# Feed-forward products by Strassen's seven products in a kernel of two transformer blocks

## The chip, the cores and the metric

The kernel runs on one core of a Trainium2 chip as one program. The metric is the device time of one execution in microseconds (us), as a median of several runs; lower is better. PE is the matrix engine (TensorE), DVE the vector engine, ACT the scalar engine, POOL the GpSimd engine; SP issues the loads.

## What is computed

Two blocks follow each other on 512 tokens of 1024 features, in float32. Each has two gated feed-forwards around a token mixer (the mixers are left out here), and a small product follows at the end. A feed-forward normalises its input, takes 5632 columns of products from it (2816 "gate" and 2816 "up"), gates them and takes 1024 columns from those:

```python
def rms_norm(x, g):
    xf = x.astype(jnp.float32)
    y = xf * lax.rsqrt(jnp.mean(xf * xf, axis=-1, keepdims=True) + EPS)
    return (y * g.astype(jnp.float32)).astype(x.dtype)

def swiglu_ffn(x, w_in, w_out):
    gate, up = jnp.split(x @ w_in, 2, axis=-1)
    return (jax.nn.silu(gate) * up) @ w_out
```

The first block adds half of the normed result to x; the second adds half of the result. The four feed-forwards are called f1, f2 (block 1) and f3, f4 (block 2). Their order is f1, mixer, f2, f3, mixer, f4, and then the last product.

## The kernel before

Features lie on the 128 partitions, and the 512 tokens along the row. The input of a feed-forward is eight tiles of 128 features by 512 tokens, so a chunk of 128 columns of `w_in` takes eight steps k. A float32 product is made from parts: `split` (L306) and `wpiece` (L242) write a high part of an operand (a copy on ACT, L247 for weights, L310 and L313 for activations) and the rest, low, on DVE (L248 for weights, L311 and L314 for activations). `mm3` (L258) then issues three matmuls: high by high (L259), high weight by low input (L260), low weight by high input (L261).

`ffn` (L450) goes through 22 pairs m of a gate chunk and an up chunk. `lin` (L284) loads 512 KB of weights for a chunk on SP, makes the parts, and issues 24 matmuls of 512 columns into a PSUM bank, so a pair is 48 matmuls. The input parts are those of gain times x, without the per-token factor R, which arrives later (L393); R is multiplied in when DVE reads the bank (L463 and L464). ACT takes the Silu in place (L94), DVE multiplies gate and up (L466) and the product is split at once (L310, L311). Then the output products follow: `out_post` (L397) in f1 and f2, a loop at L472 in f3 and f4, eight chunks with 66 matmuls each (`f2o` for those of f2). The last chunk in f1 and f2 is done in two halves of 256 tokens.

The first two pairs of f1, f2 and f3 are issued ahead by `lin_ahead` (L295), also in halves of 256 columns, while the input still arrives; in f4 none is.

A tile scheduler orders the instructions of each engine by the data they need and the order in which they are written; the engines then run their lists strictly in order and wait on semaphores. Weights go through a pool of three raw buffers, four high and four low ones; other tiles of 128 by 512 come from a pool of 72. `Squares.add` (L367) sums squares on POOL (L376), which has no other large work. `late_constants` (L177) loads vectors of later stages on POOL's queue, transposes them into `pcolb`, and computes tables; in f1 it is written ahead of pair 2.

Tile names in the profile drop numbers: f_6g is the gate chunk of pair 6 in any of the feed-forwards (here the time tells which), `_r`, `_h`, `_l` are raw, high and low.

## Time and profile before

| | us |
|---|---|
| median of 3 runs (2273.32 to 2273.71) | 2273.33 |
| profiled execution, first to last instruction | 2267.5 |
| PE busy in it | 2247.1 (99%) |
| DVE busy | 1151.6 (51%) |
| ACT busy | 881.5 (39%) |
| POOL busy | 119.6 (5%) |

The span of the profiled execution is 5.8 us under the median of the times; a run's time takes in what lies before the first and behind the last instruction. The two are not told apart by the profile: differences of the span are set against the median as they are. The feed-forwards' pairs lie at 43 to 263 us (f1), 715 to 934 (f2), 1083 to 1302 (f3) and 1840 to 2082 (f4). Times of a matmul overlap: rows give a length of 0.39 us where one starts every 0.23 us, so what a matmul costs is read from start to start.

### The profile page before, as it was taken

To read this page: it belongs to the slowest core of one execution; us is meant where nothing else is said; L and a number is where in the kernel's file an instruction comes from. 1 tells how busy PE (TensorE), PEld (TensorE's weight loads), DVE (VectorE), ACT (ScalarE), POOL (GpSimd) and SP (SyncE) were. 2 spreads that over 40 slices of the span, in tenths; PEclk is the share of its full clock that TensorE was granted. 3 is DMA by queue.
4 is the path that set the end of the run, shared out by engine and by line. 5 is a ranking of instruction groups with operands and counts; after the bars stand their busy time and mean duration, and the time that the engine had idled before them with its cause. 6 is when DMAs were issued, how large, how long until landed. Compare 5 with 4: busy or idle time off the path is not lost.

```text
span 2267.5 us, 27653 instructions
## 1 busy us (share of the span) xinstructions
PE 2247.1 (99%) x11074; PEld 1870.9 (83%) x11074; DVE 1151.6 (51%) x1938; ACT 881.5 (39%) x1344; POOL 119.6 (5%) x156
## 2 busy tenths in 40 slices
PE   8999999999999999999999999999999999999999
PEld 7888888888788888889888888877778888888887
DVE  5644323778648444325644433476674654444334
ACT  4323223556635333223432322566654442233222
POOL 3000001000112000001000001000000010000000
PEclk9999999999889999999999999999999999999999
DMA  5333333322112333332333333321131233333331
GB/s 151 93 96 100 95 94 91 88 62 75 38 47 85 102 93 102 93 96 73 112 93 101 89 96 104 85 66 48 46 89 34 79 112 94 102 93 96 96 107 65
DMA packets 364836, 197.22 MB, mean 87 GB/s; under 512 B 10007, under 2 KB 356516, under 8 KB 364708
## 3 DMA queue, kind: packets, MB, share of 16 engines
q1 hardware_dynamic: 364100, 195.37, 30.0%
q8 instruction: 87, 1.43, 0.3%
q0 software_dynamic: 608, 0.09, 0.0%
q14 instruction: 41, 0.34, 0.0%
HBM read 193.33 MB, written 2.10 MB: 86 GB/s over the span
## 4 chain that ended last, share of the span: by engine, by line
PE 98%; DVE 1%; ACT 0%; DMA 0%; issue 0%; SPq 0%; DVEq 0%
PE f1o_p L260 2%; PE f2o_p L259 2%; PE f2o_p L260 2%; PE f1o_p L259 2%; PE f2o_p L261 2%; PE f1o_p L261 2%; PE f4o_p L259 2%; PE f3o_p L261 2%; PE f4o_p L261 2%; PE f3o_p L259 2%; PE f3o_p L260 2%; PE f4o_p L260 2%; PE gt_p L260 1%; PE gt_p L259 1%; PE gt_p L261 1%; PE f_p L260 1%
## 5 line engine op out<-in xcount | busy, mean ns | idle before, releaser
L248 DVE TENSOR_TENSOR f1o_l<-f1o_r,f1o_h 128x1024 fp32r<-128x1024 f32 (+1 forms) x24 | 27.3, 1136 | 76.6 <-ACT f1o_h L247 76.6
L248 DVE TENSOR_TENSOR f2o_l<-f2o_r,f2o_h 128x1024 fp32r<-128x1024 f32 (+1 forms) x24 | 27.3, 1136 | 76.6 <-ACT f2o_h L247 76.6
L247 ACT ACTIVATE f2o_h<-f2o_r 128x1024 fp32r<-128x1024 f32 (+1 forms) x24 | 23.8, 990 | 85.7 <-PE f2o_p L260 73.0
L247 ACT ACTIVATE f1o_h<-f1o_r 128x1024 fp32r<-128x1024 f32 (+1 forms) x24 | 23.8, 990 | 85.7 <-PE f1o_p L260 68.4
L247 ACT ACTIVATE f3o_h<-f3o_r 128x1024 fp32r<-128x1024 f32 (+1 forms) x24 | 23.8, 990 | 85.3 <-PE f3o_p L260 53.2
L247 ACT ACTIVATE f4o_h<-f4o_r 128x1024 fp32r<-128x1024 f32 (+1 forms) x24 | 23.8, 990 | 85.0 <-PE f4o_p L260 52.8
L376 POOL TENSOR_TENSOR f_acc<-f_acc,f_sq 128x256 f32<-128x256 f32 (+1 forms) x42 | 38.9, 927 | 316.9 <-ACT f_sq L375 299.5
L248 DVE TENSOR_TENSOR f3o_l<-f3o_r,f3o_h 128x1024 fp32r<-128x1024 f32 (+1 forms) x24 | 27.3, 1136 | 54.0 <-ACT f3o_h L247 54.0
L248 DVE TENSOR_TENSOR f4o_l<-f4o_r,f4o_h 128x1024 fp32r<-128x1024 f32 (+1 forms) x24 | 27.3, 1135 | 52.5 <-ACT f4o_h L247 52.5
L84 ACT ACT_TABLE_LOAD x36 | 46.2, 1283 | 1.4 <-PEq L1341 0.8
L376 POOL TENSOR_TENSOR m_acc<-m_acc,m_sq 128x256 f32<-128x256 f32 (+1 forms) x18 | 20.1, 1115 | 348.8 <-ACT m_sq L375 348.8
L260 PE MATMUL m1o_p<-mix_l,m1o_h 128*128 128x256 f32 (+1 forms) x88 | 29.3, 334 | 0.0
L261 PE MATMUL m1o_p<-mix_h,m1o_l 128*128 128x256 f32 (+1 forms) x88 | 29.2, 334 | 0.0
L259 PE MATMUL m1o_p<-mix_h,m1o_h 128*128 128x256 f32 (+1 forms) x88 | 28.6, 336 | 0.0
L376 POOL TENSOR_TENSOR pl_acc<-pl_acc,pl_sq 128x512 f32<-128x512 f32 x6 | 10.3, 1710 | 341.6 <-ACT pl_sq L375 341.6
L248 DVE TENSOR_TENSOR gt_l<-gt_r,gt_h 128x1024 fp32r<-128x1024 f32 x16 | 19.6, 1224 | 12.9 <-ACT gt_h L247 12.6
L94 ACT ACTIVATE l<-l 128x384 f32<-128x384 f32 (+1 forms) x48 | 24.2, 554 | 3.1 <-DVE l L949 3.0
L247 ACT ACTIVATE pg_h<-pg_r 128x1024 fp32r<-128x1024 f32 x8 | 8.5, 1061 | 42.6 <-PE pp L496 19.4
L94 ACT ACTIVATE e<-ms,mx,sck 128x512 f32<-128x512 f32 (+3 forms) x32 | 19.5, 614 | 14.0 <-DVE mx L1135 13.8
L260 PE MATMUL wo_p<-mg_l,wo_h 128*128 128x512 f32 x64 | 24.8, 390 | 0.0
L259 PE MATMUL wo_p<-mg_h,wo_h 128*128 128x512 f32 x64 | 24.8, 389 | 0.0
L376 POOL TENSOR_TENSOR f2p_acc<-f2p_acc,f2p_sq 128x512 f32<-128x512 f32 x6 | 7.7, 1288 | 322.9 <-ACT f2p_sq L375 322.9
(4287 smaller groups left out, 7533.5 us busy)
## 6 DMA issues: line engine op xcount, KB each, us to landing
f1o_r<-in_ffn_w_out_dram SPq DMA_DIRECT2D x16, 512.0 KB, 3.8
f2o_r<-in_ffn_w_out_dram SPq DMA_DIRECT2D x16, 512.0 KB, 4.3
f3o_r<-in_ffn_w_out_dram SPq DMA_DIRECT2D x16, 512.0 KB, 4.3
gt_r<-in_w_in_dram SPq DMA_DIRECT2D x16, 512.0 KB, 4.0
f4o_r<-in_ffn_w_out_dram SPq DMA_DIRECT2D x16, 512.0 KB, 4.1
f_r<-in_ffn_w_in_dram SPq DMA_DIRECT2D x12, 512.0 KB, 5.0
mg_r<-in_w_mix_in_dram SPq DMA_DIRECT2D x8, 512.0 KB, 4.0
m1o_r<-in_w_mix_out_dram SPq DMA_DIRECT2D x8, 512.0 KB, 4.2
```

The costliest lines, as they stand in the source:

```text
L84: ld = S.preload_act_table_set(name).ins
L94: i = S.activation(out, in_, func, **kw).ins
L247: S.activation(hi, raw, AF.Copy)
L248: V.tensor_tensor(lo, raw, hi.bitcast(F32), ALU.subtract)
L259: M.matmul(o, w[0], u[0], start=first, stop=False)
L260: M.matmul(o, w[0], u[1], start=False, stop=False)
L261: issued["last"] = M.matmul(o, w[1], u[0], start=False, stop=last).ins.name
L376: G.tensor_tensor(acc[:, sl], acc[:, sl], q[:, sl], ALU.add)
```

## The change

Pairs 0 to 5 of each feed-forward stay as they are (called direct). Pairs 6 to 21 are made by the Winograd form of Strassen's method: the weights of a pair and the input are cut into 2 by 2 blocks (k halves by gate and up; k halves by token halves), and seven products of blocks take the place of eight. A product of blocks is four steps k of three matmuls with 256 columns; a pair is 84 of these instead of 48 of 512.

The seven products need seven forms of the normed input (`b11`, `b21`, `n1`, `t3`, `t2`, `b22`, `t4`), each in four tiles with high and low parts. `strassen_input` makes them among the direct pairs: eight products of x, gain and R on DVE (the forms hold R, so R is not multiplied into the results), 16 sums and differences of 256 columns on DVE, 28 high parts on ACT and 28 low parts on DVE.

`strassen_pair` loads the two chunks of a pair raw (r0, r1), and makes four weight forms from them: a = r0, b = s1 (the two halves of r1 added, 512 columns), c = r0's first half added into r1, and d (s1 added into r0's first half, and that into its second half). The four additions, 128 by 512 each, are on POOL; of each form ACT makes the high part and DVE the low part. The results come together in two banks, `ab` and `cd`: ACT copies two halves (`s`), and DVE makes five sums of 256 columns (`o1`, `o2`). Silu and product of gate and up follow as before.

All 22 products are split behind the last pair and no longer pair by pair. `late_constants` is written behind the pairs of f1, `norm_post` is loaded at the very start on SP and taken out of it. There is one raw weight buffer more, and two tiles fewer in the pool.

```diff
+NDIRECT = 6
+HT = T // 2
+HK = KD // 2
...
-    act = ctx.enter_context(tc.tile_pool(name="act", bufs=72))
-    wraw = ctx.enter_context(tc.tile_pool(name="wraw", bufs=3))
+    act = ctx.enter_context(tc.tile_pool(name="act", bufs=70))
+    wraw = ctx.enter_context(tc.tile_pool(name="wraw", bufs=4))
...
     def late_constants():
-        load_rows(["norm_post", "ffn1_norm_2", "mix_norm_2", "ffn2_norm_2", "ple_norm_2", "hgrn_norm", "mlstm_norm",
+        load_rows(["ffn1_norm_2", "mix_norm_2", "ffn2_norm_2", "ple_norm_2", "hgrn_norm", "mlstm_norm",
                    "conv_w", "conv_b", "hgrn_lb_logits", "q_latent_norm_2", "kv_latent_norm_2"], "b", nc.gpsimd)
-        for i, j in ((0, 0), (1, 2)):
-            V.tensor_scalar(gph[:, i * KD:(i + 1) * KD], cols("norm_post", j * KD, KD), 0.5, None, ALU.mult)
         V.tensor_copy(identb, ident)
         ii, jj, xx, gt_ = (A(f"ix{i}", I32, (P, P)) for i in range(4))
...
+    def mm3(o, w, u, first, last, more=False):
...
+    def strassen_input(x, nx, R, between):
+        un, forms = [None] * KD, [{} for _ in range(HK)]
+        def normed(k):
+            un[k] = A(f"{nx.name}_n{k}")
+            V.scalar_tensor_tensor(un[k], x[k], nx.g(k), R, ALU.mult, ALU.mult)
+        def form(k, name, src, sign=1.0):
+            t = A(f"{nx.name}_{name}{k}", F32R)
+            hi, lo = t[:, 0:HT], t[:, HT:]
+            S.activation(hi, src, AF.Copy, scale=sign)
+            if sign > 0:
+                V.tensor_tensor(lo, src, hi.bitcast(F32), ALU.subtract)
+            else:
+                V.scalar_tensor_tensor(lo, src, sign, hi.bitcast(F32), ALU.mult, ALU.subtract)
+            forms[k][name] = hi, lo
+        between(0)
+        for k in range(KD):
+            normed(k)
+            form(k % HK, "b21" if k >= HK else "b11", un[k][:, 0:HT])
+        between(1)
+        d1, d2 = [], []
+        for k in range(HK):
+            b11, b12, b22 = un[k][:, 0:HT], un[k][:, HT:], un[HK + k][:, HT:]
+            d1.append(A(f"{nx.name}_d1{k}"))
+            V.tensor_tensor(d1[k][:, 0:HT], b12, b11, ALU.subtract)
+            V.tensor_tensor(d1[k][:, HT:], b22, b12, ALU.subtract)
+            form(k, "n1", d1[k][:, 0:HT], -1.0)
+            form(k, "t3", d1[k][:, HT:])
+        between(2)
+        for k in range(HK):
+            b21, b22 = un[HK + k][:, 0:HT], un[HK + k][:, HT:]
+            d2.append(A(f"{nx.name}_d2{k}"))
+            V.tensor_tensor(d2[k][:, 0:HT], b22, d1[k][:, 0:HT], ALU.subtract)
+            V.tensor_tensor(d2[k][:, HT:], d2[k][:, 0:HT], b21, ALU.subtract)
+            form(k, "t2", d2[k][:, 0:HT], -1.0)
+        between(3)
+        for k in range(HK):
+            form(k, "b22", un[HK + k][:, HT:])
+            form(k, "t4", d2[k][:, HT:])
+        return forms
 
+    def strassen_pair(w, c0, c1, forms, name, done):
+        r0, r1 = (wraw.tile([P, KD, P], F32, tag="raw", name=f"{name}_r{i}") for i in range(2))
+        for r, c in ((r0, c0), (r1, c1)):
+            nc.sync.dma_start(out=r, in_=w[:, c:c + P].rearrange("(k p) c -> p k c", p=P))
+        def parts(r, nm, n=KD):
+            if n == KD:
+                hi, lo = whi.tile([P, n, P], F32R, tag="hi", name=nm + "_h"), wlo.tile([P, n, P], F32R, tag="lo",
+                                                                                     name=nm + "_l")
+            else:
+                hi, lo = (act.tile([P, n, P], F32R, tag="a", name=f"{nm}_{j}") for j in "hl")
+            S.activation(hi, r, AF.Copy)
+            V.tensor_tensor(lo, r, hi.bitcast(F32), ALU.subtract)
+            return [(hi[:, k, :], lo[:, k, :]) for k in range(n)]
+        first, last = slice(0, HK), slice(HK, KD)
+        g1 = parts(r0, name + "a")
+        s1 = act.tile([P, HK, P], F32, tag="a", name=name + "_s1")
+        G.tensor_tensor(s1, r1[:, first], r1[:, last], ALU.add)
+        g2 = parts(s1, name + "b", HK)
+        G.tensor_tensor(r1[:, first], r0[:, first], r1[:, first], ALU.add)
+        g3 = parts(r1, name + "c")
+        G.tensor_tensor(r0[:, first], r0[:, first], s1, ALU.add)
+        G.tensor_tensor(r0[:, last], r0[:, last], r0[:, first], ALU.add)
+        g4 = parts(r0, name + "d")
+        def product(o, ws, form, start, stop, more=False):
+            for k in range(HK):
+                mm3(o, ws[k], forms[k][form], start and k == 0, stop and k == HK - 1, more)
+        ab, cd = ps(name + "_ab"), ps(name + "_cd")
+        (a, b), (c, d) = ((t[:, 0:HT], t[:, HT:]) for t in (ab, cd))
+        sab, o1, o2 = A(name + "_s"), A(name + "_o1"), A(name + "_o2")
+        product(a, g1[:HK], "b11", True, False)
+        product(b, g1[HK:], "b21", False, True)
+        yield
+        S.activation(sab[:, HT:], b, AF.Copy)
+        V.tensor_tensor(o1[:, 0:HT], a, sab[:, HT:], ALU.add)
+        product(c, g2, "n1", True, False)
+        product(d, g3[:HK], "t3", False, True)
+        product(a, g4[:HK], "t2", False, True, True)
+        S.activation(sab[:, 0:HT], a, AF.Copy)
+        V.tensor_tensor(o2[:, HT:], c, sab[:, 0:HT], ALU.add)
+        V.scalar_tensor_tensor(o2[:, HT:], o2[:, HT:], -1.0, d, ALU.mult, ALU.subtract)
+        yield
+        product(c, g4[HK:], "b22", False, False, True)
+        product(d, g3[HK:], "t4", False, True, True)
+        V.tensor_tensor(o1[:, HT:], c, sab[:, 0:HT], ALU.add)
+        V.scalar_tensor_tensor(o2[:, 0:HT], d, -1.0, sab[:, 0:HT], ALU.mult, ALU.subtract)
+        done(o1, o2)
+        yield
...
         us, R, _ = nx.factor()
         table("silu_and_others")
-        hs = []
-        for m in range(KF):
-            if m == 2 and name == "f1":
-                late_constants()
+        hs = [None] * KF
+        def direct(m):
             n = f"{name}_{m}"
-            pg = lin(w_in, m * P, us, n + "g")
-            pu = lin(w_in, DFF + m * P, us, n + "u")
-            gr, ur = A(n + "gr"), A(n + "ur")
+            return lin(w_in, m * P, us, n + "g"), lin(w_in, DFF + m * P, us, n + "u")
+        def gated(m, gr, ur):
+            lut(gr, gr, AF.Silu)
+            V.tensor_tensor(ur, gr, ur, ALU.mult)
+            hs[m] = ur
+        def evict(m, pg, pu):
+            gr, ur = A(f"{name}_{m}gr"), A(f"{name}_{m}ur")
             V.tensor_tensor(gr, pg, R, ALU.mult)
             V.tensor_tensor(ur, pu, R, ALU.mult)
-            lut(gr, gr, AF.Silu)
-            V.tensor_tensor(ur, gr, ur, ALU.mult)
-            hs.append(split(ur, n + "h"))
+            gated(m, gr, ur)
+        ready = {m: direct(m) for m in range(3)}
+        def between(i):
+            for m in ((0, 1), (2,), (3,), ())[i]:
+                evict(m, *ready.pop(m))
+            if i < 3:
+                ready[3 + i] = direct(3 + i)
+        forms = strassen_input(x, nx, R, between)
+        for m in range(4, NDIRECT):
+            evict(m, *(ready.pop(m) if m in ready else direct(m)))
+        pairs = {m: strassen_pair(w_in, m * P, DFF + m * P, forms, f"{name}_{m}",
+                                  lambda gr, ur, m=m: gated(m, gr, ur)) for m in range(NDIRECT, KF)}
+        run(pairs[NDIRECT], 1)
+        for m in range(NDIRECT, KF):
+            run(pairs[m], 1)
+            if m + 1 < KF:
+                run(pairs[m + 1], 1)
+            run(pairs[m])
+        hs = [split(hs[m], f"{name}_{m}h") for m in range(KF)]
+        if name == "f1":
+            late_constants()
...
-    load_rows(["norm_pre"], "a", nc.sync)
+    load_rows(["norm_pre", "norm_post"], "a", nc.sync)
+    for i, j in ((0, 0), (1, 2)):
+        V.tensor_scalar(gph[:, i * KD:(i + 1) * KD], cols("norm_post", j * KD, KD), 0.5, None, ALU.mult)
```

DVE's list in pairs 6 and 7 of f2 before: `gr` and `ur` are the products with R and then the gated product, `_l` the low parts of weights (8u, 9g, 9u, 10g) or of the gated product (6h, 7h).

```order
L248 TENSOR_TENSOR f2_8u_0_l_6525<-f2_8u_0_r_6522,f2_8u_0_h_6524 128x1024
L311 TENSOR_TENSOR f2_6h_l_6416<-f2_6ur_6410,f2_6h_h_6415 128x512
L463 TENSOR_TENSOR f2_7gr_6481<-f2_7g_p_6425,f2_R_6031 128x512
L248 TENSOR_TENSOR f2_9g_0_l_6566<-f2_9g_0_r_6563,f2_9g_0_h_6565 128x1024
L464 TENSOR_TENSOR f2_7ur_6482<-f2_7u_p_6456,f2_R_6031 128x512
L466 TENSOR_TENSOR f2_7ur_6482<-f2_7gr_6481,f2_7ur_6482 128x512
L248 TENSOR_TENSOR f2_9u_0_l_6597<-f2_9u_0_r_6594,f2_9u_0_h_6596 128x1024
L311 TENSOR_TENSOR f2_7h_l_6488<-f2_7ur_6482,f2_7h_h_6487 128x512
```

DVE's list now for one pair, from the low part of form d of pair 8 to that of pair 9 (`a_l` to `d_l` are low parts of weight forms, L569 is the product of gate and up):

```order
L515 TENSOR_TENSOR f2_8d_l_7691<-f2_8_r0_7669,f2_8d_h_7690 128x1024
L515 TENSOR_TENSOR f2_9a_l_7797<-f2_9_r0_7792,f2_9a_h_7796 128x1024
L569 TENSOR_TENSOR f2_7_o2_7575<-f2_7_o1_7574,f2_7_o2_7575 128x512
L545 TENSOR_TENSOR f2_8_o2_7698<-f2_8_cd_7695,f2_8_s_7696 128x256
L546 SCALAR_TENSOR_TENSOR f2_8_o2_7698<-f2_8_o2_7698,f2_8_cd_7695 128x256
L515 TENSOR_TENSOR f2_9b_l_7803<-f2_9_s1_7800,f2_9b_h_7802 128x512
L540 TENSOR_TENSOR f2_9_o1_7820<-f2_9_ab_7817,f2_9_s_7819 128x256
L515 TENSOR_TENSOR f2_9c_l_7808<-f2_9_r1_7793,f2_9c_h_7807 128x1024
L550 TENSOR_TENSOR f2_8_o1_7697<-f2_8_cd_7695,f2_8_s_7696 128x256
L551 SCALAR_TENSOR_TENSOR f2_8_o2_7698<-f2_8_cd_7695,f2_8_s_7696 128x256
L515 TENSOR_TENSOR f2_9d_l_7814<-f2_9_r0_7792,f2_9d_h_7813 128x1024
L515 TENSOR_TENSOR f2_10a_l_7920<-f2_10_r0_7915,f2_10a_h_7919 128x1024
```

Each pair has its three large low parts (a, c, d) and one of 512 columns (b); the two products with R are gone, and five operations of 256 columns stand between the low parts. The low part of d of a pair comes directly ahead of that of a of the next pair.

PE's list now, where pair 8's product t2 (which reads form d) begins and pair 9's first product (form a) is let in:

```order
L260 MATMUL f2_8_ab_7694<-f2_t20_7394,f2_8d_h_7690 128x256
L261 MATMUL f2_8_ab_7694<-f2_t20_7394,f2_8d_h_7690 128x256
L260 MATMUL f2_9_ab_7817<-f2_b110_7181,f2_9a_h_7796 128x256
L261 MATMUL f2_9_ab_7817<-f2_b110_7181,f2_9a_h_7796 128x256
L262 MATMUL f2_8_ab_7694<-f2_t20_7394,f2_8d_l_7691 128x256
L260 MATMUL f2_8_ab_7694<-f2_t21_7400,f2_8d_h_7690 128x256
```

The product t2 comes 24 matmuls behind the end of pair 7's last product (t3 and n1 of pair 8 stand between), its third matmul reads `d_l` 28 behind it, and the low part of `9a` is read first 38 behind it. From t2 of one pair to t2 of the next it is 84 matmuls.

DVE's list now where f2's forms are made. Ahead of these rows stand R and the first two pairs' products with it; `n0` to `n7` are the normed tiles:

```order
L464 SCALAR_TENSOR_TENSOR f2_n1_7184<-x1_160,pcola_118,f2_R_7035 128x512
L471 TENSOR_TENSOR f2_b110_7181<-f2_n0_7179,f2_b110_7181 128x256
L464 SCALAR_TENSOR_TENSOR f2_n2_7189<-x2_161,pcola_118,f2_R_7035 128x512
L249 TENSOR_TENSOR f2_5g_0_l_7332<-f2_5g_0_r_7329,f2_5g_0_h_7331 128x1024
L464 SCALAR_TENSOR_TENSOR f2_n3_7194<-x3_162,pcola_118,f2_R_7035 128x512
L471 TENSOR_TENSOR f2_b111_7186<-f2_n1_7184,f2_b111_7186 128x256
L471 TENSOR_TENSOR f2_b112_7191<-f2_n2_7189,f2_b112_7191 128x256
L464 SCALAR_TENSOR_TENSOR f2_n4_7199<-x4_163,pcola_118,f2_R_7035 128x512
L471 TENSOR_TENSOR f2_b113_7196<-f2_n3_7194,f2_b113_7196 128x256
```

Line numbers in the lists of the changed kernel are its own. From the copy of R to the low part of `6b`, the second weight form that the first Strassen pair needs, DVE's list now has 75 rows; before, 25 rows led from R to the low part of `6u`, which had that place.

DVE's list now at the end of f2's pairs (`f2o0` is the first chunk of the output weights, `0h` the split of the gated product of pair 0):

```order
L249 TENSOR_TENSOR f2o0_0_l_9513<-f2o0_0_r_9510,f2o0_0_h_9512 128x1024
L569 TENSOR_TENSOR f2_20_o2_9174<-f2_20_o1_9173,f2_20_o2_9174 128x512
L249 TENSOR_TENSOR f2o0_8_l_9519<-f2o0_8_r_9516,f2o0_8_h_9518 128x1024
L545 TENSOR_TENSOR f2_21_o2_9297<-f2_21_cd_9294,f2_21_s_9295 128x256
L312 TENSOR_TENSOR f2_0h_l_9420<-f2_0ur_7106,f2_0h_h_9419 128x512
L312 TENSOR_TENSOR f2_1h_l_9424<-f2_1ur_7112,f2_1h_h_9423 128x512
L546 SCALAR_TENSOR_TENSOR f2_21_o2_9297<-f2_21_o2_9297,f2_21_cd_9294 128x256
L312 TENSOR_TENSOR f2_2h_l_9428<-f2_2ur_7220,f2_2h_h_9427 128x512
```

The low parts of the splits begin behind the sum L545 that waits for pair 21's product t2, where before 21 of 22 splits lay among the pairs. On PE the first seven matmuls of `f2o0` stand between pair 21's t2 and its last two products.

## Rows read from the trace of the kernel before

**Rows 1.** The page's parts 1 and 4: busy time; the chain that ended last.

```profile
PE 2247.1 (99%) x11074; PEld 1870.9 (83%) x11074; DVE 1151.6 (51%) x1938; ACT 881.5 (39%) x1344; POOL 119.6 (5%) x156
...
PE 98%; DVE 1%; ACT 0%; DMA 0%; issue 0%; SPq 0%; DVEq 0%
```

**Rows 2.** Windows: f2's 20 pairs, R to pair 6; busy of five engines, PEclk, DMA.

```profile
715.30:933.50 218.20, 218.20 (x966) 180.74 (x967) 107.50 (x134) 71.09 (x89) 0.00 (x0) 1.00 0.35 103
724.80:759.40 34.60, 34.60 (x155) 28.63 (x154) 21.38 (x29) 12.68 (x17) 0.00 (x0) 1.00 0.39 112
```

**Rows 3.** Timeline of PE, pair 6 of f2: start, length, engine, line, operation.

```profile
759.39 0.39 PE L259 MATMUL f_6g_p<-f_u0h,f_6g_h 128*128 128x512 f32 x1
...
770.27 0.39 PE L259 MATMUL f_7g_p<-f_u0h,f_7g_h 128*128 128x512 f32 x1
```

**Rows 4.** Window in f3's first pairs, done in halves of 256 columns: PE alone.

```profile
1062.00:1080.00 18.00, 18.00 (x149) 1.00 0.00 1
```

**Rows 5.** Timeline of PE, last output chunk of f2, second half.

```profile
1046.69 0.28 PE L259 MATMUL f2o_p<-f_1h_h,f2o_h 128*128 128x256 f32 x1
...
1047.29 0.28 PE L261 MATMUL f2o_p<-f_2h_h,f2o_l 128*128 128x256 f32 x1
```

**Rows 6.** Timeline of DVE, pair 6 of f2.

```profile
760.39 0.69 DVE L466 TENSOR_TENSOR f_5ur<-f_5gr,f_5ur 128x512 f32<-128x512 f32 x1
761.00 1.22 DVE L248 TENSOR_TENSOR f_7u_l<-f_7u_r,f_7u_h 128x1024 fp32r<-128x1024 f32 x1
762.13 0.69 DVE L311 TENSOR_TENSOR f_5h_l<-f_5ur,f_5h_h 128x512 fp32r<-128x512 f32 x1
```

**Rows 7.** Timeline of ACT, pair 6 of f2.

```profile
764.85 1.06 ACT L247 ACTIVATE f_8g_h<-f_8g_r 128x1024 fp32r<-128x1024 f32 x1 [3.11 <-PE f_6g_p L260]
```

**Rows 8.** Timeline of DVE ahead of f2, 256 columns.

```profile
705.70 0.43 DVE L440 TENSOR_TENSOR x<-x,m_y 128x256 f32<-128x256 f32 x1
706.05 0.96 DVE L314 SCALAR_TENSOR_TENSOR f_u3l<-x,pcola,f_u3h 128x256 fp32r<-128x256 f32 x1
...
708.07 0.47 DVE L314 SCALAR_TENSOR_TENSOR f_u4l<-x,pcola,f_u4h 128x256 fp32r<-128x256 f32 x1
708.47 0.41 DVE L439 TENSOR_TENSOR m_y<-m_y,m1p 128x256 f32<-128x256 f32 x1
```

**Rows 9.** Timeline of POOL at the same place.

```profile
705.94 0.79 POOL L376 TENSOR_TENSOR f_acc<-f_acc,f_sq 128x256 f32<-128x256 f32 x1 [1.28 <-ACT f_sq L375]
```

**Rows 10.** The page's part 5: POOL's additions of 512 columns.

```profile
L376 POOL TENSOR_TENSOR pl_acc<-pl_acc,pl_sq 128x512 f32<-128x512 f32 x6 | 10.3, 1710 | 341.6 <-ACT pl_sq L375 341.6
...
L376 POOL TENSOR_TENSOR f2p_acc<-f2p_acc,f2p_sq 128x512 f32<-128x512 f32 x6 | 7.7, 1288 | 322.9 <-ACT f2p_sq L375 322.9
```

**Rows 11.** Timelines of POOL and DVE in the first mixer's output product.

```profile
666.80 2.82 POOL L376 TENSOR_TENSOR m1p_acc<-m1p_acc,m1p_sq 128x512 f32<-128x512 f32 x2 [0.78 <-ACT m1p_sq L375]
668.70 2.00 DVE L248 TENSOR_TENSOR m1o_l<-m1o_r,m1o_h 128x1024 fp32r<-128x1024 f32 x1 [1.60 <-ACT m1o_h L247]
```

**Rows 12.** Line L314 by tile: count; least, median, most ns; forms.

```profile
L314 DVE SCALAR_TENSOR_TENSOR f_u4l<-x,pcolb,f_u4h x3: 472/472/739, 1064.0 to 1826.2; 128x256 fp32r<-128x256 f32 x2, 128x512 fp32r<-128x512 f32 x1
```

**Rows 13.** Timeline of ACT ahead of f2, 256 columns.

```profile
706.58 0.40 ACT L375 ACTIVATE f_sq<-x 128x256 f32<-128x256 f32 x1
```

**Rows 14.** DMA issues from 700 to 760 us: KB each, us to landing.

```profile
f_4u_r<-in_ffn_w_in_dram SPq DMA_DIRECT2D x1, 512.0 KB, 6.1
```

**Rows 15.** Timeline of DVE when f2's factor R arrives.

```profile
724.81 0.69 DVE L393 COPY f_R<-f_sp 128x512 f32<-128x512 f32 x1
```

**Rows 16.** Timelines of PE and DVE where f2's output product begins.

```profile
933.47 0.39 PE L259 MATMUL f2o_p<-f_0h_h,f2o_h 128*128 128x512 f32 x1
936.21 0.69 DVE L311 TENSOR_TENSOR f_21h_l<-f_21ur,f_21h_h 128x512 fp32r<-128x512 f32 x1
```

**Rows 17.** Waits of PE: total us, times, longest.

```profile
PE f_5g_p L259 <- DVE f_2gr L463: 1.4, 1, 1.4
```

More of the change, by code (lines that the diff above doesn't have):

```diff
@@ L256, in wcols @@
         return r
-    def mm3(o, w, u, first, last):
-        M.matmul(o, w[0], u[0], start=first, stop=False)
-        M.matmul(o, w[0], u[1], start=False, stop=False)
-        issued["last"] = M.matmul(o, w[1], u[0], start=False, stop=last).ins.name
+    def mm3(o, w, u, first, last, more=False):
+        M.matmul(o, w[0], u[0], start=first, stop=False, skip_group_check=more)
+        M.matmul(o, w[0], u[1], start=False, stop=False, skip_group_check=more)
+        issued["last"] = M.matmul(o, w[1], u[0], start=False, stop=last, skip_group_check=more).ins.name
     issued = {}
```

## The prediction

> **What bounds the kernel now.** Read the page first: PE is busy 99% of the span and makes 98% of the chain that ended last; DVE is busy 51%, ACT 39%, POOL 5% [rows 1]. So only what changes PE's own time, or makes PE wait, counts. The windows say the same of the stage concerned: in f2's twenty pairs PE is busy 218.20 of 218.20 us at PEclk 1.00, which is 2.4 GHz, DVE 107.50 [rows 2]. PE's timeline then gives the price of a pair: the first matmuls of pairs 6 and 7 start 10.88 us apart, for 48 matmuls of 512 columns, 226.7 ns each [rows 3].
>
> **PE's new price.** Matmuls of 256 columns with a weight load each stand in the trace: 149 in 18.00 us, 120.8 ns each [rows 4], and six starts from 1046.69 to 1047.29, 120 ns each [rows 5]. A pair of 84 costs 10.08 to 10.15 us; I take 10.12. That is more than half of 512's price, so the method's eighth shrinks to 0.76 us a pair. For 64 pairs: **-48.8 us** (bounds -46.7 and -51.2).
>
> **Steady pairs.** DVE's list for a pair has three low parts of 1024 columns (1.22 us each by length, 1.13 from start to start), one of 512 and the gated product (0.69; 0.61) [rows 6], and five operations of 256 columns (0.41 to 0.47; 0.35 to 0.40) [rows 8]: 7.2 us by length, under 10.12. The tight place is product t2. Form d of a pair goes into the weight buffer that t4 of the pair before has just left, so its high part starts only then: 1.06 us on ACT [rows 7], then 1.22 on DVE, 2.3 with some hand-over, and PE asks for it 28 matmuls, 3.36 us, later. The low part of the next a follows at 3.5 and is asked for after 38 matmuls, 4.56 us. About 1 us of cover each; PE waits only if something else holds DVE up.
>
> That can be POOL. DVE's 256-column operation took 0.96 instead of 0.47 us when POOL had begun an addition 0.11 us before [rows 8, 9], and a low part of 1024 columns took 2.00 instead of 1.22 beside POOL's pair of additions [rows 11, 6]. So an addition holds up a DVE operation with two inputs in SBUF, and one of 512 columns costs POOL 1.29 us alone, 1.71 where it has company [rows 10]. Four additions a pair are 5.2 us; the five DVE operations with two SBUF inputs are 3 x 1.22 + 2 x 0.69 = 5.0. Fully exclusive by length that is **10.2 us, as long as PE's pair**; by start-to-start times 4.6 + some 4.6 = 9.2. The five sums read PSUM and may lie beside additions. By the lists, two additions wait for the low part of a and come after the tight pair of low parts, and two wait for the loads of a next pair, in mid-period; a collision costs the gated product or c, which have 1 to 2 us of cover. Bounds per pair: 0 (all covered) and 0.4 us (one addition of 1.29 in front of d, less 0.9 of cover). I take 0.1, nearest the covered end, as the lists avoid the place: **+6.4 us** (0 to 25.6).
>
> The Trainium skill ("SBUF — State Buffer", section "SBUF: two separate sides") says that DVE and GpSimd share a port pair as an exclusive lock, held for the whole instruction, also against a DVE operation with two SBUF inputs. The 0.96 us [rows 8] agrees; a lock on full lengths would make the pair 10.2 us and speaks against this change.
>
> **Start of the pairs.** R is copied at 724.81 in f2 [rows 15], and pair 6 starts at 759.39 [rows 3]; its b form is needed 26 matmuls later, at 762.5. PE goes through the direct pairs as before. DVE must by then do 75 operations: a copy and 18 of 512 columns (0.69; 0.61), eight normed tiles of 512 (0.74 [rows 12]; about 0.66), four low parts of 1024 (1.22; 1.13), 36 operations of 256 and eight of the other kind (0.41, 0.47; 0.35, 0.40) [rows 6, 8]. From start to start: 11.6 + 5.3 + 4.5 + 12.6 + 3.2 = 37.2 us, done at 762.0; by length 13.1 + 5.9 + 4.9 + 14.8 + 3.8 = 42.5, done at 767.3. Up to six of POOL's additions fall there, up to 7.7 us. Before, DVE was busy 21.38 of the 34.60 us [rows 2]; this slack is gone. Late by 0 to 12 us; I take 4, start-to-start times with three additions in the way. f1 and f3 have the same list; f4 has no pairs ahead, its pair 6 starts two pairs later after R, so 0. **+12 us** (0 to 36).
>
> **End of the pairs.** Before, 21 of 22 splits lay among the pairs; the last took DVE at 936.21 while PE was already in f2o from 933.47 on [rows 16]. Now DVE makes 22 in a row at 0.61 to 0.69 us. PE's first matmul of f2o comes behind pair 21's t2 and needs split 0: ACT's copy of 256 columns (0.40) [rows 13], its high part (0.5), then DVE's 0.69: 1 to 2.5 us of waiting. Then a step k of f2o takes PE 3 x 0.227 = 0.68, about DVE's pace, but weight parts of 1.22 stand in between; PE has 24 matmuls of pair 21 and the next chunk's in reserve. Bounds 1 and 5 a feed-forward, taken 2.5: **+10 us** (4 to 20).
>
> **Smaller edits.** Moved behind f1's pairs, `late_constants` no longer makes PE wait 1.4 us for pair 5 [rows 17]; its loads on POOL's queue stand behind the last additions, its DVE work behind f1's splits, under 120 us of f1o: **-1.4** (to 0). `norm_post` on SP is one small load more ahead of the first weights, 0 to 1 us: **+0.5**. A fourth raw buffer lets loads start sooner; 512 KB landed in up to 6.1 us with several in flight [rows 14], against two loads in 10 us now as before: 0. Two tiles fewer in the pool: 0, unless splits wait for forms to be freed, which is within the end's bounds. The scheduler's small swaps in the mixers: 0, within 3 either way.
>
> **Sum:** -48.8 + 6.4 + 12 + 10 - 1.4 + 0.5 = -21.3 us. The profiled execution is 2267.5 + 5.8 us around it, the median 2273.33; I set the difference against the median: **2252 us**. All favourable bounds give -51.2 + 0 + 0 + 4 - 1.4 + 0 = -48.6, or 2225; all unfavourable ones -46.7 + 25.6 + 36 + 20 + 1 = +36, or 2309.
>
> **The rivals.**
> 1. *Covers hold.* DVE keeps up at the start by start-to-start times, additions fall between, and only the ends cost 4 to 10 us: 2226 to 2236. For it: DVE's busy share of 51% [rows 1]. Against: 37.2 us of list in a 37.7 us window. Chance 0.2.
> 2. *Starts and ends take most.* DVE is late by 10 us in f1, f2, f3 and PE waits 4 at each end: -48.8 + 6.4 + 30 + 16 - 1 = +2.6 in the worst case, 2262 to 2276. Additions beside forms speak for it [rows 8, 9]. Chance 0.15.
> 3. *The pair becomes DVE's and POOL's: slower.* The two exclude each other for 10.2 us by length, and half of the five sums (2.1 us by length) can't be laid beside additions: 11.3 us a pair, 0.4 over the old one, 64 x 0.4 = +27, with starts and ends +22: 2322. It decides once a pair is over 10.88 - 22/64 = 10.5 us, that is 0.4 of waiting in each. For it: 1.71 us additions [rows 10], 2.00 us low parts [rows 11]. Against: 9.2 us by start to start, and a loop that can slide DVE's work under PE's 10.12. Chance 0.1.
> 4. *The change doesn't do what it says.* PE would issue 48 by 512 as before; the lists show the 84, so 0.02, with 2273.
>
> **How the numbers follow.** The forecast, 2237 to 2261, has 0.53, the rivals 0.2, 0.15, 0.1 and 0.02. Faster, same and slower are set apart by 0.2% (4.5 us, about what a measurement of this kernel can tell from no change). Faster takes the forecast, rival 1 and two thirds of rival 2: 0.83. Same: a third of that less a bit, and rival 4: 0.05. Slower: rival 3 and the worst of 2: 0.12. The range runs from 2226 to 2282: it cuts off rival 3's price and the lowest edge of rival 1.
>
> **What would show it.** In the changed profile: starts of t2 from pair to pair (10.1 right, 10.5 or more is rival 3); PE's idle time ahead of the first `ab` and `cd` products of f1, f2, f3, released by DVE, 4 us each; ahead of `f2o` 2 to 3 us, released by L312 or L311; POOL's additions at 1.3 to 1.8 us and low parts at 1.2 to 2. Wrong would be a PE that waits in every pair, a clock under 1.00 in the pairs, or a 256-column start-to-start time that is not 0.12.

## The result, and the profile after

The change takes **2246.43 us** (median of 4 runs, 2242.81 to 2246.50) against 2273.52 for the kernel before; the ratio is 0.9885, 95% interval 0.9865 to 0.9906. That is 27.1 us less, where 21.3 less were forecast. The profiled execution has a span of 2240.7 us, 26.8 under that of before.

Parts 1 and 4 of the page of the changed kernel, which answer to [rows 1]:

```profile
PE 2204.4 (98%) x13378; PEld 1943.6 (87%) x13378; DVE 1461.5 (65%) x2466; ACT 1044.7 (47%) x1712; POOL 505.6 (23%) x411
...
PE 94%; DVE 4%; ACT 1%; DMA 0%; SPq 0%; issue 0%; DVEq 0%; ACTq 0%
```

PE is busy 42.7 us less, DVE 309.9 us more and POOL 386.0 us more; PE's share of the chain fell from 98% to 94%, and DVE's rose from 1% to 4%. PE has some waits it did not have. The waits of PE (total us, times, longest):

```profile
PE f_cd L262 <- DVE f_6b_l L515: 11.0, 3, 4.3
...
PE pcola L153 <- DMA prowa<-in_norm_post_dram: 2.6, 1, 2.6
...
PE f_cd L262 <- DVE f_6c_l L515: 1.1, 2, 0.8
...
PE f1o_p L260 <- ACT f_0h_h L311: 1.0, 1, 1.0
...
PE f4o_p L260 <- ACT f_0h_h L311: 1.0, 1, 1.0
```

The largest is where it was looked for: the low part of `6b` at the start of the pairs in f1, f2 and f3. Each output product waits 1.0 us for its first split. Of the pairs only pair 6, the first, stands in the list.

For the steady pairs, the start of product n1 of three pairs in f2, on PE's timeline:

```profile
782.07 0.28 PE L260 MATMUL f_cd<-f_n,f_8b_h 128*128 128x256 f32 x1
...
792.15 0.28 PE L260 MATMUL f_cd<-f_n,f_9b_h 128*128 128x256 f32 x1
...
802.23 0.28 PE L260 MATMUL f_cd<-f_n,f_10b_h 128*128 128x256 f32 x1
```

10.08 us from pair to pair, twice, which is 84 times 120 ns. In f1, f2, f3 and f4 every interval but the first is 10.08, to 0.01 us. A window over pairs 7 to 20 of f4 (busy us of PE, weight loads, DVE, ACT, POOL; PEclk; DMA):

```profile
1905.50:2046.70 141.20, 141.20 (x1179) 141.20 (x1178) 108.89 (x142) 66.86 (x99) 82.46 (x55) 1.00 0.37 105
```

PE has no gap at clock 1.00, though DVE is busy 77% and POOL 58% of that time; before, DVE was busy for half of it [rows 2].

By stages the difference is as follows. A stage of pairs runs from the first matmul of pair 6 (with seven direct pairs, of pair 7) to the first of the output product, read from PE's timeline; all are us.

| stage | before | change | no additions | late forms | no normed tiles | seven direct (15 pairs) |
|---|---|---|---|---|---|---|
| f1 pairs | 174.1 | 164.6 | 162.2 | 164.3 | 160.9 | 150.8 |
| f2 pairs | 174.1 | 165.4 | 163.9 | 162.8 | 160.8 | 150.8 |
| f3 pairs | 174.1 | 163.7 | 162.9 | 162.9 | 160.9 | 150.8 |
| f4 pairs | 174.1 | 160.9 | 160.9 | 162.5 | 160.8 | 150.8 |

Without any waiting the stage of the change would be 1320 matmuls (24 of the 1344 come behind the output's first ones) of 0.12 us and 1.15 us for the output's first wait: 159.6. The rest is the cost of the start: 5.1, 5.9, 4.2 and 1.3 us, **16.4** together. That is more than the 12.1 us that PE waited there for `6b` and `6c`; a part of the difference is its clock (below). The output products with the last 24 matmuls, and that first wait, cost 1.8 to 2.0 us more than before in each feed-forward, **7.4** together.

### The profile page after: what moved, and what is told of

The parts are those of the page before. It is cut to its first block, busy times and chain, and to the rows that moved or that the text cites. A ratio compares the mean times of both kernels' runs of the same rounds, so it can differ in the third digit from the quotient of the medians.

```text
span 2240.7 us, 33637 instructions
## 1 busy us (share of the span) xinstructions
PE 2204.4 (98%) x13378; PEld 1943.6 (87%) x13378; DVE 1461.5 (65%) x2466; ACT 1044.7 (47%) x1712; POOL 505.6 (23%) x411
## 4 chain that ended last, share of the span: by engine, by line
PE 94%; DVE 4%; ACT 1%; DMA 0%; SPq 0%; issue 0%; DVEq 0%; ACTq 0%
PE f_cd L262 6%; PE f_cd L261 5%; PE f_cd L260 5%; PE f_ab L262 4%; PE f_ab L261 4%; PE f_ab L260 4%; PE f1o_p L261 2%; PE f2o_p L261 2%; PE f4o_p L261 2%; PE f1o_p L262 2%; PE f1o_p L260 2%; PE f2o_p L262 2%; PE f2o_p L260 2%; PE f3o_p L261 2%; PE f3o_p L262 2%; PE f4o_p L262 2%
## 5 line engine op out<-in xcount | busy, mean ns | idle before, releaser
L525 POOL TENSOR_TENSOR f_r<-f_r,f_s 128x512 f32<-128x512 f32 x64 | 100.8, 1576 | 218.2 <-issue 32.9
L521 POOL TENSOR_TENSOR f_s<-f_r 128x512 f32<-128x512 f32 x64 | 92.8, 1450 | 226.1 <-PE f_5u_p L261 137.2
L544 ACT ACTIVATE f_s<-f_ab 128x256 f32<-128x256 f32 x64 | 24.6, 384 | 210.2 <-PE f_ab L262 210.2
L523 POOL TENSOR_TENSOR f_r<-f_r,f_r 128x512 f32<-128x512 f32 x64 | 108.3, 1692 | 5.0
L526 POOL TENSOR_TENSOR f_r<-f_r 128x512 f32<-128x512 f32 x64 | 83.4, 1304 | 5.0
L539 ACT ACTIVATE f_s<-f_ab 128x256 f32<-128x256 f32 x64 | 24.6, 384 | 121.4 <-PE f_ab L262 121.4
L545 DVE TENSOR_TENSOR f_o<-f_cd,f_s 128x256 f32<-128x256 f32 x64 | 27.2, 424 | 60.9 <-ACT f_s L544 60.9
L97 ACT ACTIVATE f_o<-f_o 128x512 f32<-128x512 f32 x64 | 40.5, 632 | 22.3 <-DVE f_o L550 19.5
L540 DVE TENSOR_TENSOR f_o<-f_ab,f_s 128x256 f32<-128x256 f32 x64 | 27.1, 424 | 35.8 <-ACT f_s L539 35.8
L569 DVE TENSOR_TENSOR f_o<-f_o,f_o 128x512 f32<-128x512 f32 x64 | 43.4, 678 | 0.0
L377 POOL TENSOR_TENSOR cq_acc<-cq_acc,cq_sq 128x512 f32<-128x512 f32 x1 | 1.3, 1292 | 160.8 <-ACT cq_sq L376 160.8
```

The costliest lines, as they stand in the source:

```text
L377: G.tensor_tensor(acc[:, sl], acc[:, sl], q[:, sl], ALU.add)
L521: G.tensor_tensor(s1, r1[:, first], r1[:, last], ALU.add)
L523: G.tensor_tensor(r1[:, first], r0[:, first], r1[:, first], ALU.add)
L525: G.tensor_tensor(r0[:, first], r0[:, first], s1, ALU.add)
L526: G.tensor_tensor(r0[:, last], r0[:, last], r0[:, first], ALU.add)
L569: V.tensor_tensor(ur, gr, ur, ALU.mult)
```

## The experiments

Times of one kernel differ by up to 12.5 us from run to run here, and in two profiled executions of the change nearly all of the difference lies in the first mixer (last section). So the stages above, which agree to 0.2 us between these two executions, carry the verdicts; the medians stand beside them. The clock behind a wait can still move a stage by 1 to 2 us, which is said where it does.

**The start: what makes `6b` late?** DVE's timeline in f2 when pair 5 ends and pair 6 begins:

```profile
750.97 0.68 DVE L574 TENSOR_TENSOR f_5gr<-f_5g_p,f_R 128x512 f32<-128x512 f32 x1
751.58 0.92 DVE L471 TENSOR_TENSOR f_t<-f_d,f_t 128x256 fp32r<-128x256 f32 x1
752.42 1.51 DVE L471 TENSOR_TENSOR f_b<-f_n,f_b 128x256 fp32r<-128x256 f32 x1
753.85 1.51 DVE L471 TENSOR_TENSOR f_t<-f_d,f_t 128x256 fp32r<-128x256 f32 x1
...
758.12 0.41 DVE L471 TENSOR_TENSOR f_b<-f_n,f_b 128x256 fp32r<-128x256 f32 x1
...
760.00 0.68 DVE L515 TENSOR_TENSOR f_6b_l<-f_s,f_6b_h 128x512 fp32r<-128x512 f32 x1
```

and POOL's:

```profile
748.41 2.27 POOL L521 TENSOR_TENSOR f_s<-f_r 128x512 f32<-128x512 f32 x1 [43.95 <-PE f_5u_p L261]
...
753.73 1.35 POOL L526 TENSOR_TENSOR f_r<-f_r 128x512 f32<-128x512 f32 x1
...
756.59 1.33 POOL L523 TENSOR_TENSOR f_r<-f_r,f_r 128x512 f32<-128x512 f32 x1
```

Five of the last forms take 0.92 to 1.51 us instead of 0.41 while POOL makes six additions, with gaps of no more than 0.1 us, from 748.41 to 757.92. DVE had not been idle for more than 0.4 us since R. The low part of `6b` starts at 760.00 and PE, which wanted it at 756.4, waits 4.3 us. Two theories: the additions' lock does it, or DVE's list is too long by itself.

PE's clock is a part of the cost that neither theory names. Behind the wait in f2 PE's timeline goes on like this,

```profile
760.73 0.58 PE L262 MATMUL f_cd<-f_n,f_6b_l 128*128 128x256 f32 x1 [4.31 <-DVE f_6b_l L515]
761.11 0.41 PE L260 MATMUL f_cd<-f_n,f_6b_h 128*128 128x256 f32 x1
761.32 0.41 PE L261 MATMUL f_cd<-f_n,f_6b_h 128*128 128x256 f32 x1
```

0.21 us from start to start instead of 0.12, and windows behind the waits in f1, f2 and f3 have a PEclk of 0.54, 0.52 and 1.00:

```profile
94.60:98.30 3.70, 3.70 (x18) 3.70 (x19) 3.70 (x5) 0.00 (x0) 0.00 (x0) 0.54 0.16 45
760.70:763.90 3.20, 3.17 (x15) 3.17 (x16) 3.20 (x5) 0.00 (x0) 0.00 (x0) 0.52 0.03 8
1124.00:1127.00 3.00, 2.63 (x20) 2.43 (x21) 3.00 (x5) 0.00 (x0) 0.00 (x0) 1.00 0.01 3
```

In f1 and f2 the granted clock fell to the lower of its two levels, 1.2 GHz; in f3, whose wait for `6b` was as long as f1's (3.3 us), it did not. So f1's start costs 0.9 us more than f3's. For f2 the same sum gives an estimate of 0.7: 5.9, less f3's 4.2, less a wait that is 1.0 longer. The other start-up waits below are read with this in mind.

*Additions left out*:

```diff
-        G.tensor_tensor(s1, r1[:, first], r1[:, last], ALU.add)
-        g2 = parts(s1, name + "b", HK)
-        G.tensor_tensor(r1[:, first], r0[:, first], r1[:, first], ALU.add)
+        g2 = parts(r1[:, first], name + "b", HK)
         g3 = parts(r1, name + "c")
-        G.tensor_tensor(r0[:, first], r0[:, first], s1, ALU.add)
-        G.tensor_tensor(r0[:, last], r0[:, last], r0[:, first], ALU.add)
         g4 = parts(r0, name + "d")
```

> The four additions on POOL per pair are left out (form b is r1's first half, c is r1, d is r0), so the pairs' weights are not the method's; all else stays. Theory: without the lock the forms' tail takes 0.41 us each, 6b is ready 5 us sooner, and the 11 us of waiting ahead of pair 6 in f1, f2, f3 vanish (0 to 2 us left); the steady pairs stay at 10.08 us, since the lock was covered there; time about 2235.5 (2233 to 2238). Rival (the lock costs nothing, the wait is DVE's own list): the 11 us stay, time 2246. Rival (the lock also costs in the steady pairs): pairs shorter than 10.08 us.

2237.93 us (2231.82 to 2238.95). The wait on `6b` is gone, but the stages fall by 4.7 us together, not by 11, and some 1.6 of the 4.7 is the clock by the estimate above: it was 1.00 in all pairs here. Its waits of PE show what came in its place:

```profile
PE f_ab L262 <- DVE f_7a_l L515: 4.4, 3, 1.7
PE f_cd L260 <- ACT f_7b_h L514: 3.9, 4, 1.0
```

DVE is now late with `7a`, ACT with `7b`. DVE's timeline in f2 shows why:

```profile
754.39 0.41 DVE L471 TENSOR_TENSOR f_t<-f_d,f_t 128x256 fp32r<-128x256 f32 x1
754.73 1.22 DVE L515 TENSOR_TENSOR f_7a_l<-f_r,f_7a_h 128x1024 fp32r<-128x1024 f32 x1
755.87 0.68 DVE L515 TENSOR_TENSOR f_6b_l<-f_r,f_6b_h 128x512 fp32r<-128x512 f32 x1
...
763.09 1.23 DVE L515 TENSOR_TENSOR f_7d_l<-f_r,f_7d_h 128x1024 fp32r<-128x1024 f32 x1 [3.87 <-PE f_ab L262]
```

Every form takes 0.41 us, where five took 0.92 to 1.51 in the change: 4.9 us less, which is the lock's price in f2. But from R (at 716.45 here) to the low part of `6b` it is 39.4 us, only 1.8 less than in the change. For the list is sorted anew without the additions: three low parts of 1024 columns (`6c`, `6d`, `7a`; 1.14 us each from start to start) now stand ahead of it, and one sum of 0.60 behind it. PE is let into pair 7's first product early and waits there, and DVE is idle for 3.87 us at 763.09, so its load is not what binds by then. The run shows what the lock costs, which is more than the 4.3 us that PE waited for `6b`; it doesn't show that the start's 16.4 us would go without it, since the order changed with it. The steady pairs stay at PE's price, so the lock costs nothing there.

*Forms b22 and t4 written later*, behind pair 7's weight forms:

```diff
-        for k in range(HK):
-            form(k, "b22", un[HK + k][:, HT:])
-            form(k, "t4", d2[k][:, HT:])
-        return forms
+        def late():
+            for k in range(HK):
+                form(k, "b22", un[HK + k][:, HT:])
+                form(k, "t4", d2[k][:, HT:])
+        return forms, late
...
                 run(pairs[m + 1], 1)
+            if m == NDIRECT:
+                late()
```

> The forms b22 and t4 are written behind pair 7's first weight forms instead of ahead of pair 6; nothing else moves. Theory (the 11.0 us that PE waits for the low part of 6b in f1, f2 and f3 come from POOL's six additions, which lock the last forms of DVE's list, 1.5 instead of 0.41 us each, ahead of 6b): 6b is ready some 5 us sooner, the 11.0 us fall to 0 to 4, of which some may come back as waits for b22, t4, 6c or 6d; time about 2237 (2234 to 2241). Rival (DVE's list is simply too long, whatever its order): the wait moves to 6c, 6d or the forms, and the time stays within 2 us of 2246.4.

2240.20 us (2236.27 to 2243.51). The stages give 2.1 us, with 1.6 lost in f4. Its waits of PE:

```profile
PE f_cd L261 <- DVE f_b L471: 4.0, 3, 1.4
...
PE f_cd L262 <- DVE f_6c_l L518: 2.3, 3, 0.8
...
PE f_cd L262 <- DVE f_6b_l L518: 0.7, 1, 0.7
```

The wait on `6b` fell from 11.0 to 0.7, but 4.0 came at the forms (f_b), 2.3 instead of 1.1 at `6c`, and 0.9 in pairs 7 and 8 of f4. PE's waits in the pairs fell from 12.1 to 7.9 us together, with more short stops beside them; the clock was 0.51 over 104.9 to 108.3 us in f1 and 1.00 in f2's pairs. The median lies in the range of the theory, but the stages, which carry the verdict, gain 2.1 us, no more than the clock can move. So this is nearer to the rival: the order moves most of the wait and does not remove it.

*No normed tiles*:

```diff
-            un[k] = A(f"{nx.name}_n{k}")
-            V.scalar_tensor_tensor(un[k], x[k], nx.g(k), R, ALU.mult, ALU.mult)
+            un[k] = x[k]
```

> The eight products of x, gain and R are left out and the forms made of x itself, so the pairs of the method lack the norm; DVE's list ahead of pair 6 is 8 x 0.66 = 5.3 us shorter, the rest and POOL's additions stay. Theory (the start is late because DVE's list, lengthened by the additions' lock, overruns its window of 37.7 us): in f1, f2 and f3 the time from pair 6 to the output product falls to f4's 160.9 us or near it (within 0.5), 14 us less in all; time about 2233 plus what the first mixer varies. Rival (the high parts on ACT or the late additions set the start): the stages of f1 to f3 stay at 163.7 to 165.4 us.

2235.37 us (one run). 160.85, 160.80, 160.85 and 160.79: all four feed-forwards are alike now. 5.3 us less of DVE's list, with all additions still made, take 3.8, 4.6 and 2.9 us off f1, f2 and f3: 11.2 together, where 14 was expected, with the clock's share in it. Four of the six additions came some 10 us sooner in f2, beside other operations, but five operations of the list were held up by 4.9 us in all, as in the change. So it is the sum that overruns the window: the list, and the lock's 4.9 us in it. By these sums about 5 us less of either would do for `6b`; for the list it is shown, for the lock worked out.

*Seven direct pairs* (`NDIRECT = 7`), which gives DVE 10.9 us more:

> Seven direct pairs instead of six, so 15 pairs of each feed-forward by the method. Theory: DVE's list has 10.9 us more ahead of the first Strassen pair, the forms are done before POOL's additions begin, and the 11 to 12 us of waiting in f1, f2, f3 vanish; four pairs cost 0.80 us each, 3.2: 2246.4 - 11.5 + 3.2 = 2238 (2235 to 2242). Rival (the additions always fall into the forms' tail, since they wait for a tile that the last direct pair gives up): the waits stay, 2249.6.

2238.77 us (2230.34 to 2241.12); ratio to the kernel before 0.9845 (0.9823 to 0.9868). The forms were not done before the additions, as was expected: in f2 three of them were met again and took 1.09 to 1.51 us, but the longer window covers that. Each stage of 15 pairs takes 150.78 us where 15 times 10.08, less 24 matmuls, and the 1.15 of the output make 149.5. One wait is left, once in each feed-forward, 0.8 us:

```profile
PE f_cd L262 <- DVE f_7c_l L515: 3.0, 4, 0.8
```

It is the same 1.3 us that f4 loses in the change. There the sum for `6c` was ready early on POOL,

```profile
1885.61 1.63 POOL L523 TENSOR_TENSOR f_r<-f_r,f_r 128x512 f32<-128x512 f32 x1
```

but on ACT its high part stands behind the copy `s`, which waits for PE's second product of the pair,

```profile
1893.44 0.39 ACT L539 ACTIVATE f_s<-f_ab 128x256 f32<-128x256 f32 x1 [5.51 <-PE f_ab L262]
1893.72 1.05 ACT L514 ACTIVATE f_6c_h<-f_r 128x1024 fp32r<-128x1024 f32 x1
```

and PE asks before the low part is there:

```profile
1896.08 0.39 PE L262 MATMUL f_cd<-f_t,f_6c_l 128*128 128x256 f32 x1 [0.76 <-DVE f_6c_l L515]
```

A feature of ACT's list for the first pair, then, and not of DVE's load. Without the additions, where the lists are sorted anew, it is gone, but f4 waits 1.0 us for the high part of `7b` instead.

**The steady pairs: how far is the lock from binding?** In f2, DVE meets POOL's addition of pair 7 like this,

```profile
770.67 2.17 DVE L515 TENSOR_TENSOR f_7c_l<-f_r,f_7c_h 128x1024 fp32r<-128x1024 f32 x1 [0.52 <-ACT f_7c_h L514]
...
773.43 1.21 DVE L515 TENSOR_TENSOR f_7d_l<-f_r,f_7d_h 128x1024 fp32r<-128x1024 f32 x1
774.57 1.21 DVE L515 TENSOR_TENSOR f_8a_l<-f_r,f_8a_h 128x1024 fp32r<-128x1024 f32 x1
```

```profile
770.47 1.29 POOL L523 TENSOR_TENSOR f_r<-f_r,f_r 128x512 f32<-128x512 f32 x1
775.92 1.61 POOL L525 TENSOR_TENSOR f_r<-f_r,f_s 128x512 f32<-128x512 f32 x1 [4.16 <-DVE f_8a_l L515]
```

POOL began at 770.47 and DVE's low part of `7c` at 770.67: it ends 1.08 us behind POOL's end, about the time of a whole low part. But the next, `7d` and `8a`, the tight place of the prediction, find POOL idle, and POOL's next addition waits for `8a`. So here the list falls as it was read. Over pairs 8 to 21 of the four feed-forwards it is looser: c is held up in 40 of 56, d in 13 (up to 1.66 us instead of 1.22), a once (2.32), and b, which the prediction did not name, in all 56 (0.73 to 1.76 instead of 0.68). PE waits for none of them, so the cover holds in the tight place too.

*Eight additions a pair* (the first one issued five times):

```diff
-        G.tensor_tensor(s1, r1[:, first], r1[:, last], ALU.add)
+        for _ in range(5):
+            G.tensor_tensor(s1, r1[:, first], r1[:, last], ALU.add)
```

> The first addition of every pair is issued five times, so POOL makes eight a pair instead of four; the result is the same. Theory (an addition and a DVE operation with two SBUF inputs exclude each other for nearly their whole length): a pair takes the sum, 8 x 1.15 to 1.38 us of POOL plus 4.3 to 5.0 of DVE, 13.5 to 16 us; 64 pairs over 10.08 give 2246 + 219 to 379, about 2540. Rival (they share, each some slower): POOL alone bounds the pair, 8 x 1.38 = 11.0 us, time about 2246 + 60 = 2306.

2612.08 us (one run), 72 more than expected; a pair in f4 takes 15.1 to 16.9 us, where full exclusion was to make 13.5 to 16. But the number does not price the lock by itself. POOL's timeline and DVE's in a pair (x3 is three additions in one row):

```profile
2347.54 4.30 POOL L522 TENSOR_TENSOR f_s<-f_r 128x512 f32<-128x512 f32 x3
...
2357.04 1.29 POOL L526 TENSOR_TENSOR f_r<-f_r,f_s 128x512 f32<-128x512 f32 x1 [3.50 <-DVE f_18a_l L515]
```

```profile
2350.64 1.75 DVE L515 TENSOR_TENSOR f_17b_l<-f_s,f_17b_h 128x512 fp32r<-128x512 f32 x1
...
2354.55 1.21 DVE L515 TENSOR_TENSOR f_17d_l<-f_r,f_17d_h 128x1024 fp32r<-128x1024 f32 x1
```

A low part of 512 columns took 1.75 instead of 0.69 us, yet POOL was idle for 3.5 us of the 16 while it waited for DVE's `18a`, and again for a load. The four more additions all stand ahead of form b, 1.37 us each from start to start, 5.5 us on the way from the load to b; and it is b that PE waits for, 129.9 us for its low part and 103.0 for its high part over the four feed-forwards. So a longer way to b is a rival to the lock as the cause, and the run does not tell them apart; the clock fell too (last section). The pair is a ring of additions, high and low parts, freed buffers and loads, and the lock is a part of it. What it shows safely: with four more additions ahead of b the cover is gone and each pair is 5 to 7 us longer; with the four of the change it holds.

**The end: splits 0 and 1 early**

```diff
+            if m + 3 == KF:
+                early = [split(hs[j], f"{name}_{j}h") for j in range(2)]
             run(pairs[m])
-        hs = [split(hs[m], f"{name}_{m}h") for m in range(KF)]
+        hs = early + [split(hs[m], f"{name}_{m}h") for m in range(2, KF)]
```

The place in the change, on PE's timeline and on ACT's in f2:

```profile
918.58 0.49 PE L260 MATMUL f2o_p<-f_0h_h,f2o_h 128*128 128x512 f32 x1 [0.99 <-ACT f_0h_h L311]
919.30 0.50 PE L261 MATMUL f2o_p<-f_0h_l,f2o_h 128*128 128x512 f32 x1 [0.23 <-DVE f_0h_l L312]
```

```profile
917.62 0.38 ACT L544 ACTIVATE f_s<-f_ab 128x256 f32<-128x256 f32 x1 [2.27 <-PE f_ab L262]
917.90 0.62 ACT L311 ACTIVATE f_0h_h<-f_0ur 128x512 fp32r<-128x512 f32 x1
```

ACT copies `s` and makes split 0, PE waits 1.0 and 0.2 us.

> The splits of pairs 0 and 1 are written ahead of pair 20's last step instead of behind all pairs. Theory (PE waits 1.2 us at each first output chunk for ACT's high part and DVE's low part of split 0, which stand behind pair 21's product t2): these waits vanish in all four feed-forwards, 4.8 us less in the stages of the output products and the pairs before them; time about 2241.6. Rival (the wait moves to split 2 or to the output weights): under 2 us.

2244.87 us (2241.67 to 2245.47). In f4 pairs and output products together take 283.86 us, as in the change (283.85); the sum over all four is 0.6 us longer, but that holds the clock too, which stayed at 1.00 in f1's pair 6 and fell in f3's (0.50 over 1123.6 to 1130.2 us, from within a wait of 4.3 us for `6b`), so f4 is the one to compare. The 1.0 us waits are gone, and others came: 0.2 us for split 2, on PE's timeline in f4,

```profile
2055.95 0.50 PE L261 MATMUL f4o_p<-f_2h_l,f4o_h 128*128 128x512 f32 x1 [0.22 <-DVE f_2h_l L312]
```

and up to 0.3 us in pair 20 where the early splits stand on DVE. The rival was right, by f4: the wait moves.

**The price of a narrow matmul, by itself.** The kernel before, with each direct chunk computed in two halves of 256 tokens (`for sl in HALVES` around the loop over k in `lin`):

> The kernel before, with every direct gate and up chunk computed in two halves of 256 tokens: 96 matmuls of 256 columns a pair instead of 48 of 512, nothing saved. Prices the narrower matmul by itself. Theory: 96 x 0.120 = 11.52 us a pair, 0.64 more for 82 pairs, 52 us: about 2326. Rival (the weight load of each matmul bounds it at the 0.19 us that it lasts): 96 x 0.19 = 18.2 us a pair, 2870.

2324.72 us (one run). f2's twenty pairs take 231.05 us from the first matmul to the output product's first, where they took 218.2 [rows 2]: 0.64 a pair. PE's timeline in pair 8:

```profile
799.50 0.28 PE L259 MATMUL f_8g_p<-f_u0h,f_8g_h 128*128 128x256 f32 x1
...
800.46 0.28 PE L261 MATMUL f_8g_p<-f_u2h,f_8g_l 128*128 128x256 f32 x1
```

Eight steps of 0.12 us. So the method saves an eighth of 96 narrow matmuls, 1.44 us a pair, and 0.64 of that pays for their being narrow.

**Versions that might be faster.** Seven direct pairs in f1 to f3, six in f4, splits 0 and 1 early and `norm_post` loaded behind the first weights:

> Seven direct pairs in f1, f2, f3 and six in f4, splits 0 and 1 early, and norm_post loaded behind the first weights (its own rows and transpose). By the theory of the two waits: against the run with seven direct pairs -0.8 in f4, -4.8 at the four ends, -0.5 at the start: about 2232.5, span about 2231, and PE idle in the four feed-forwards under 6 us in all. Rival (the additions or the tile pool bring a new wait): 2238 or more.

2233.87 us (2226.93 to 2239.42). The feed-forwards' stages, direct pairs and outputs included, take 1342.7 us, as with seven direct pairs alone (1342.8). The pairs and outputs by themselves take 1140.6 against 1142.9: the 0.8 us of f4 was gained, and the ends gave some 1.5, not 4.8. But f1's direct pairs take 1.6 us more, with the clock at 0.57 over 45 to 49 us, those of f2 and f3 0.6 more, and the start of the program was no shorter, since the first loads landed later in this run. The lower median is not its stages' doing. So the two edits were dropped:

> Seven direct pairs in f1, f2 and f3, six in f4, nothing else. Theory: against the change the starts give back 3.7, 4.6 and 2.9 us and cost 0.80 each: -8.8 us, and f4 stays as it was; ratio to the change 0.996. Rival (the run-to-run difference of the first mixer covers it): no difference that can be told.

> The change as it is, again, beside the run with seven and six direct pairs and on the same chip: 2246 less or more some 4 us; the seven-six kernel 8 to 9 us faster than this one.

On the same chip, 2237.77 us (2234.11 to 2239.23, ratio 0.9848, 0.9826 to 0.9871) against 2242.48 (2241.52 to 2249.00, ratio 0.9877, 0.9855 to 0.9900) for the change. The intervals overlap; the stages don't: 1341.9 against 1351.1 us, 9.2 less where 8.8 were expected, of which some 1.6 is again the clock in f1's and f2's pair 6 of the change. Seven and six direct pairs beat the change by the stages, and by 4.7 us in the medians shown, where 8 to 9 were expected.

## Why the prediction was right

The mechanism was right in kind: PE's price of a narrow matmul makes the gain, DVE beside POOL's additions takes some of it back where the pairs start, and the steady pairs cover the lock. That the sum is off by only 5.5 us is in part luck: the start cost 4.4 more than forecast, and the three other large terms 11.4 less. One of its own signs of being wrong did come, a clock under 1.00 in the pairs, in pair 6 of f1 and f2 alone. Term by term, of the span's -26.8 us:

| term | forecast | measured |
|---|---|---|
| PE's price of 64 pairs | -48.8 | -51.2 |
| waits in steady pairs | +6.4 | 0 |
| start of the pairs | +12 | +16.4 |
| end of the pairs | +10 | +7.4 |
| smaller edits and the rest | -0.9 | +0.6 |
| sum | -21.3 | -26.8 |

**PE's price** was right but for the choice inside its bounds: 10.08, the closer row [rows 5], not the 10.12 between it and a window that held a few other gaps [rows 4]. (64 times the 0.76 of the text is 48.6, not 48.8.)

**Steady pairs** were read rightly, with the lock and with its cover; the 0.1 us a pair, taken as a precaution, was nowhere. The place was mostly the one named, c; b was met always, and d in 13 pairs of 56, within its cover. The port rule of the Trainium skill ("SBUF — State Buffer", "SBUF: two separate sides") is borne out by the 2.17 us of `7c`. The 10.2 us a pair that full lengths would make did not come about, since additions run beside the five sums that read PSUM and beside DVE's waits: the first of these sums takes 0.42 us in the 51 pairs in which an addition overlaps it, and 0.42 in the other 13.

**The start** was sized at 4 us each and cost 5.1, 5.9 and 4.2. The wait itself was sized well: 3.3, 4.3 and 3.3 us for `6b`. From R at 718.77 to the end of `6b` at 760.68 it took 41.9 us in f2, between the 37.2 and 42.5 of the text. Three points were off: six additions fell there, not three, at 4.9 us in all; f4, put at 0, lost 1.3 to ACT's order, and f3 another 0.6 for `6c`; and the clock that fell behind the wait in f1 and f2, some 1.6 us, was no term of the sum. The place, `6b`, and its releaser, DVE, were right.

**The end** had the right wait, 1.2 us at split 0, with less behind it than 2.5. The high part that the text puts at 0.5 us without a row takes 0.62 here (`0h` above).

**Smaller edits.** PE's wait of 1.4 us for pair 5 [rows 17] is gone, and f1's direct pairs are 1.75 us shorter. The start is 0.5 longer, as forecast, since PE's wait of 2.6 us for `norm_post` mostly took the place of waiting for x (7.9 us before, 4.9 now). The rest is 1.9 us: 1.06 ahead of f3, where the clock was 0.57 over 1047 to 1051 us, 0.4 in f2's direct pairs and 0.4 in the first mixer.

Rival 3 (DVE and POOL as the bound) fell for four additions; the run with eight has longer pairs, but does not show that the lock is why. Rival 1 was closer than its chance of 0.2 says: the steady pairs did hold, and only the starts kept the time from it.
